# One start modulo 512 bytes for the matmul operands of a decoder layer, full-height compressed and last-block products, q and k turned before they are split

## The chip, the cores and the metric

The kernel runs on one core of a Trainium2 chip. The metric is the device time of one execution in microseconds (us); the lower the better. Times called ns are thousandths of that.

## The reference, cut to what matters

One layer works on 512 tokens of width 1024. The attention has 16 heads of 64, two key/value groups, and three branches: compressed blocks, selected blocks and a window. Both the selected and the window branch cover all earlier tokens at this length, so they are causal attentions with their own keys and values.

```
h = rms_norm(x, attn_norm_w);  z = h @ w_in
q, k = rope(rms_norm(q)) * SCALE, rope(rms_norm(k))       # by head, 64 wide
k_cmp, v_cmp = compress(k_c), compress(v_c)               # 31 blocks of 32 tokens
o = g0 * softmax(q k_cmp) v_cmp + g1 * softmax(q k_s) v_s + g2 * softmax(q k_w) v_w
x = x + (merge0 * (pool(u) @ w_pool_br) + merge1 * (o @ w_attn_br)) @ w_o
c = conv3(rms_norm(x, ffn_norm_w) @ w_up)                 # causal, per channel, 5504 wide
x = x + (silu(c[:2752]) * c[2752:]) @ w_down
```

## The kernel before, in words

Every fp32 product is made of rounded parts. `split` writes `hi`, the operand rounded to fp32r (ACT), and `lo`, the rest (DVE or POOL); `mm3` then runs three matmuls into one PSUM bank, `hi hi`, `hi lo` and `lo hi`, on lines 107 to 109. Transposes are matmuls of an fp32 tile with the identity `pk`.

The weights come through a ring: SP loads a 128x1024 tile `st` (2 buffers), ACT and DVE split it into 512-column tiles `hi` and `lo` (6 buffers each), TensorE (PE) uses them. All loads stand on SP's queue in program order, and each waits there until its buffer is free.

The stages, by the time at which they run:

- start to 40 us: x is loaded and split (`hh`, `hl`), the first 304 columns (`ka`), the norm.
- to about 180 us: token-major products `tg` of 256 columns for two k/v groups (`kv_group`) and four q groups (`q_group`), four token tiles each; pool mixer products `fm`, `pl`, `pb`; the compression (`ct`, `hp`, `kp`).
- to 394 us: attention, `scores` (`ss`) and `values` (`tp`, `op`) by head and branch, with the matmuls of 14 further weight tiles `fm` filled in between.
- to 441 us `w_ab` on the attention output `oT`; to 493 us `w_o` on `mh`, `ml`; to 743 us 43 tiles of `w_up` on `h2h`, `h2l` (`conv_tile`); then eight column blocks of `w_down` (`dn`) on `gh`, `gl`, with the last 64 rows of the weights kept apart (`gs`, `wlh`, `wll`).

The work of one q tile (`head_norm_rope`, `q_group`): ACT scales and squares the product, DVE and POOL make the norm and the rotation, DVE multiplies (L301). ACT writes a rounded copy into `qd` (L357), DVE the rest (L358); then PE turns four 128x128 blocks, one for each head with its two parts, into a bank `qt` of two (L361), and ACT and DVE copy two heads each out of it (L364, L365). The k tiles go the same way with four blocks (L344).

The compressed branch's product of a head has 32 rows in the contraction, in the strip of the array that the head's number sets, and runs twice, once for each part of the weights `pc` (L709):

```
for part in range(2):
    last = pe.matmul(op, Vc[32 * r:32 * r + 32, G], pc.out[part][32 * r:32 * r + 32], start=False,
                     stop=part == 1)
```

In the last block of `w_down`, L843 has all 128 rows and L844 has 64:

```
pe.matmul(ps[:, cs], wlh[:, sl], gs[:, cs], start=False, stop=False)
pe.matmul(ps[:, cs], wll[:64, sl], gs[:64, cs], start=False, stop=True)
```

Where the operands start in a partition's bytes, modulo 512 (a matmul's stationary operand and its moving one): `fm` of the early stages and of the attention 32 and 0; `w_ab` 32 and 32; `w_o` 32 and 480; `w_up` 32 and 0; `dn` 32 and 32; `tg` 0 and 32; `ss` 32 and 32; `op` 32 and 480; compressed `op` 416 and 480.

The order on each engine is set by a scheduler that goes by its own estimate of times; each engine takes its instructions in that order.

Of the kernel before, what the change touches and what calls it, by code (L numbers as in the profile page):

```python
# [19 lines left out]
P = 128  # L20
# [22 lines left out]
NKEEP = _OFF["cos"][0]  # L43

# [30 lines left out]
def layer(ctx: ExitStack, tc: tile.TileContext, par, masks, xT, w_kva, w_tm, w_fm, w_pl, w_pbr,  # L75
# [92 lines left out]
    pl_ = p1.tile([P, NPAR - NKEEP], F32, name="pl_")  # L168
# [7 lines left out]
    conv = pv("conv").rearrange("p (t c) -> p t c", c=4)  # L176
# [50 lines left out]
    for k in range(KC):  # L227
# [14 lines left out]
        if k == KC - 1:  # L242
            nc.sync.dma_start(pl_, par[:, NKEEP:])
# [38 lines left out]
    def head_norm_rope(ps, n, t, tab):  # L282
# [18 lines left out]
        v.tensor_tensor(y_, y_, rs[:, :n].unsqueeze(2).to_broadcast([P, n, DH]), ALU.mult)  # L301
        return y_
# [26 lines left out]
    def kv_group(b):  # L329
        for t, ps in tok_gemm(tm_weights(b), 256):  # L330
# [4 lines left out]
            kr = head_norm_rope(heads(ps[:, 0:128]), 2, t, 2 + b)  # L335
# [138 lines left out]
    def cmp_out(i):  # L474
# [20 lines left out]
        else:  # L495
# [6 lines left out]
            split(Vc[:, :, 0:DH], Vc[:, :, DH:P], heads(kp[:, :P]))  # L502
# [92 lines left out]
    class Cmp:  # L595
# [42 lines left out]
    work = {}  # L638

# [300 lines left out]
```

## Time and profile before

| | |
|---|---|
| time, median of 3 runs | 856.42 us (856.03 to 857.04) |
| the profiled execution's own time | 855.8 us |
| its span in the profile | 853.9 us |
| PE busy | 837.8 us, 4355 matmuls |
| DVE, ACT, POOL busy | 566.4, 466.5, 235.5 us |
| mean granted clock of PE | 0.996 |

PE's busy time counts the modelled end of each matmul, and matmuls overlap; what one costs in a stream is read from the distance of the starts, not from its duration. The span is the profile's time from the first to the last instruction.

### The profile page before, as it was taken

To read this page: it belongs to the slowest core of one execution; us is meant where nothing else is said; L and a number is where in the kernel's file an instruction comes from. 1 tells how busy PE (TensorE), PEld (TensorE's weight loads), DVE (VectorE), ACT (ScalarE), POOL (GpSimd) and SP (SyncE) were. 2 spreads that over 40 slices of the span, in tenths; PEclk is the share of its full clock that TensorE was granted. 3 is DMA by queue.
4 is the path that set the end of the run, shared out by engine and by line. 5 is a ranking of instruction groups with operands and counts; after the bars stand their busy time and mean duration, and the time that the engine had idled before them with its cause. 6 is when DMAs were issued, how large, how long until landed. Compare 5 with 4: busy or idle time off the path is not lost.

```text
span 853.9 us, 12252 instructions
## 1 busy us (share of the span) xinstructions
PE 837.8 (98%) x4355; PEld 700.9 (82%) x4355; DVE 566.4 (66%) x1203; ACT 466.5 (55%) x1002; POOL 235.5 (28%) x325
## 2 busy tenths in 40 slices
PE   7999899999999999999999999999999999999998
PEld 6889888978888888888888888888888888887887
DVE  7788967777787878785555539777777777423221
ACT  6846857768787877874334437545444444322220
POOL 5796714357565655640001200000000000000000
PEclk9999989999999999999999999999999999999999
DMA  6332132321001100101443223332233323333430
GB/s 218 102 119 91 51 102 96 103 96 50 26 26 47 30 25 26 47 28 50 148 148 99 98 74 100 99 98 83 91 100 98 99 85 104 111 108 99 111 98 25
DMA packets 22972, 72.82 MB, mean 85 GB/s; under 512 B 2816, under 2 KB 3328, under 8 KB 22912
## 3 DMA queue, kind: packets, MB, share of 16 engines
q1 hardware_dynamic: 22912, 72.05, 27.5%
q8 instruction: 34, 0.56, 0.3%
q14 instruction: 26, 0.21, 0.1%
HBM read 69.94 MB, written 2.10 MB: 84 GB/s over the span
## 4 chain that ended last, share of the span: by engine, by line
PE 84%; ACT 2%; DVE 1%; issue 1%; ACTq 0%; DVEq 0%
PE fm L107 16%; PE fm L108 16%; PE fm L109 16%; PE dn L107 5%; PE op L704 5%; PE dn L108 4%; PE dn L109 4%; PE tp L697 4%; PE ss L665 2%; PE ss L666 2%; PE op L709 1%; PE sc L608 1%; PE tg L312 1%; PE hp L461 1%; PE tg L310 1%; PE tg L311 1%
## 5 line engine op out<-in xcount | busy, mean ns | idle before, releaser
L95 ACT ACTIVATE hi<-st 128x512 fp32r<-128x512 f32 (+3 forms) x253 | 152.1, 607 | 202.2 <-PE fm L108 103.6
L98 DVE TENSOR_TENSOR lo<-st,hi 128x512 fp32r<-128x512 f32 (+1 forms) x210 | 141.8, 680 | 108.5 <-ACT hi L95 104.6
L107 PE MATMUL fm<-h2h,hi 128*128 128x512 f32 x344 | 136.1, 396 | 0.0
L108 PE MATMUL fm<-h2l,hi 128*128 128x512 f32 x344 | 136.0, 396 | 0.0
L109 PE MATMUL fm<-h2h,lo 128*128 128x512 f32 x344 | 135.9, 395 | 0.0
L677 POOL TENSOR_TENSOR pb<-pb,sm 128x128 f32<-128x128 f32 (+3 forms) x128 | 90.4, 738 | 49.3 <-DVE sm L674 40.4
L655 ACT ACTIVATE pb<-pb,nm 128x384 f32<-128x384 f32 (+3 forms) x128 | 71.1, 556 | 20.0 <-DVE nm L654 19.3
L107 PEld LDWEIGHTS fm<-h2h,hi 128*128 128x128 f32 x344 | 64.6, 188 | 15.7
L108 PEld LDWEIGHTS fm<-h2l,hi 128*128 128x128 f32 x344 | 64.6, 188 | 15.5
L109 PEld LDWEIGHTS fm<-h2h,lo 128*128 128x128 f32 x344 | 64.6, 188 | 15.5
L107 PE MATMUL fm<-hh,hi 128*128 128x512 f32 x160 | 71.6, 448 | 0.0
L107 PE MATMUL dn<-gh,hi 128*128 128x512 f32 (+1 forms) x189 | 69.9, 370 | 0.0
L108 PE MATMUL dn<-gl,hi 128*128 128x512 f32 (+1 forms) x189 | 69.1, 365 | 0.0
L109 PE MATMUL dn<-gh,lo 128*128 128x512 f32 (+1 forms) x189 | 69.1, 365 | 0.0
L98 DVE TENSOR_TENSOR ptl<-tp,pth 128x512 fp32r<-128x512 f32 (+1 forms) x96 | 57.2, 597 | 14.4 <-ACT pth L95 13.9
L654 DVE CUSTOM_DVE_ANT_0 pb<-ss,mk 128x384 f32<-128x384 f32 (+3 forms) x128 | 59.5, 482 | 8.5 <-PE ss L666 4.3
L108 PE MATMUL fm<-hl,hi 128*128 128x512 f32 x160 | 63.6, 397 | 0.0
L109 PE MATMUL fm<-hh,lo 128*128 128x512 f32 x160 | 63.0, 396 | 0.0
L95 ACT ACTIVATE pth<-tp 128x512 fp32r<-128x512 f32 (+1 forms) x96 | 49.8, 518 | 20.1 <-PE tp L697 19.7
L98 POOL TENSOR_TENSOR lo<-st,hi 128x512 fp32r<-128x512 f32 x36 | 48.5, 1350 | 34.4 <-ACT hi L95 34.4
L310 PE MATMUL tg<-hi,hh 128*128 128x256 f32 x192 | 54.1, 284 | 1.1 <-ACT h L288 1.1
L311 PE MATMUL tg<-hi,hl 128*128 128x256 f32 x192 | 53.6, 282 | 0.0
(256 smaller groups left out, 1838.4 us busy)
## 6 DMA issues: line engine op xcount, KB each, us to landing
st<-in_w_up SPq DMA_DIRECT2D x43, 512.0 KB, 3.5
st<-in_w_dn SPq DMA_DIRECT2D x24, 448.0 KB, 3.4
st<-in_w_fm SPq DMA_DIRECT2D x20, 512.0 KB, 3.5
st<-in_w_tm SPq DMA_DIRECT2D x12, 512.0 KB, 3.5
st<-in_w_ab SPq DMA_DIRECT2D x8, 512.0 KB, 3.4
st<-in_w_o SPq DMA_DIRECT2D x8, 512.0 KB, 3.5
x<-in_xT SPq DMA_DIRECT2D x15, 256.0 KB, 3.7
st<-in_cw SPq DMA_DIRECT2D x4, 512.0 KB, 3.7
```

Of the source, the lines that this page charges most:

```text
L95: a.activation(hi, src, AF.Copy)
L98: (eng or v).tensor_tensor(lo, src, r32(hi), ALU.subtract)
L107: pe.matmul(ps, sh, mh_, start=first and i == 0, stop=False)
L108: pe.matmul(ps, sh, ml_, start=False, stop=False)
L109: pe.matmul(ps, sl, mh_, start=False, stop=last and i == n - 1)
L310: pe.matmul(ps[:, :n], hh[k][:, tt], H, start=k == 0, stop=False)
L311: pe.matmul(ps[:, :n], hl[k][:, tt], H, start=False, stop=False)
L654: v.tensor_tensor_reduce(p_, ps, mcaus[:, S - n:], -1.0, 3e38, ALU.add, ALU.min, nm_[:, i:i + 1])
L655: a.activation(p_, p_, AF.Exp, bias=nm_[:, i:i + 1], scale=-1.0, accum_out=sm[:, i:i + 1])
L677: g.tensor_tensor(pb[:, PBASE[i]:PBASE[i] + n], pb[:, PBASE[i]:PBASE[i] + n], sm[:, i:i + 1].to_broadcast([P, n]), ALU.mult)
L697: last = pe.transpose(tp[:, n:n + P], pb[:, PBASE[i] + j * P:PBASE[i] + (j + 1) * P], ident)
L704: pe.matmul(op[:, j * P:], V2[b][j][:, G], pt_[:, TBASE[j]:TBASE[j] + w], start=b == 0 and j == 0 and part == 0, stop=False)
```

## The change

Tiles are placed in memory in another order, and `conv` leaves the constants' tile, so that both operands of nearly all wide matmuls start at 352 modulo 512: `tg`, `fm`, `pb`, `ss`, `op`, `w_ab`, `w_o`, `w_up` and `dn` have 352 and 352. Left elsewhere are the compressed branch (`pc` 480 on `Vc` 352; three of four windows of `Kc`), `hp`, `pl` and the identity.

`conv` is a tile of its own, loaded when the memory of the mixer is free. `Vc` gets 128 rows for each parity of the head, zero in the rows of other heads, and `pc` holds for a pair of heads the rounded part and the rest in one tile, so that a head has one matmul of 128 rows. `wll` and `gs` are used with all 128 rows. q and k are turned as fp32, two blocks for four heads (or for k's two groups), and split after it; the q bank now takes two token tiles.

```diff
 _PAR = [
-    ("ident", 128), ("fn", 8), ("psc", 4), ("conv", NFT * 4), ("b1", 2), ("vrow", 1),
+    ("ident", 128), ("fn", 8), ("psc", 4), ("b1", 2), ("vrow", 1),
     ("cos", 128), ("sin", 128), ("nw", 256), ("pos", 32), ("icnt", 64),
+    ("conv", NFT * 4),
 ]
...
     cp = pool(ctx, "cp")
+    ypp = pool(ctx, "ypp")
     xp = pool(ctx, "xp")
-    ypp = pool(ctx, "ypp")
...
+    Vc = kvp.tile([P, 2, 2, P], F32R, name="Vc")
+    g.memset(r32(Vc), 0.0)
     Kc = kvp.tile([P, 608], F32R, name="Kc")
     g.memset(r32(Kc), 0.0)
-    Vc = kvp.tile([P, 2, P], F32R, name="Vc")
...
-        v.tensor_tensor(y_, y_, rs[:, :n].unsqueeze(2).to_broadcast([P, n, DH]), ALU.mult)
-        return y_
+        rb = rs[:, :n].unsqueeze(2).to_broadcast([P, n, DH])
+        if out is None:
+            v.tensor_tensor(y_, y_, rb, ALU.mult)
+            return y_
+        o, form = out
+        v.tensor_tensor(o, form(y_), form(rb), ALU.mult)
...
-            HL = pp.tile([P, 2, 2, 2, DH], F32R, tag="kq", name=nm("kd"), bufs=KQ)
-            krb = kr[:, 0:2].unsqueeze(2).to_broadcast([P, 2, 2, DH])
-            a.activation(HL[:, 0], krb, AF.Copy)
-            v.tensor_tensor(HL[:, 1], krb, r32(HL[:, 0]), ALU.subtract)
+            k2 = pp.tile([P, 2, 2, DH], F32, tag="kq", name=nm("kd"), bufs=KQ)
...
-            for j in range(2):
-                for G in range(2):
-                    o = (2 * j + G) * P
-                    pe.transpose(tp[:, o:o + P], r32(HL[:, j, G]).rearrange("p a d -> p (a d)"), ident)
-            a.activation(KHL[:, b].rearrange("p j G s -> p (j G) s")[:, :, t * P:(t + 1) * P],
-                         tp.rearrange("p (c q) -> p c q", q=P), AF.Copy)
+            for G in range(2):
+                pe.transpose(tp[:, G * P:(G + 1) * P], k2[:, G].rearrange("p a d -> p (a d)"), ident)
+            tt = slice(t * P, (t + 1) * P)
+            split(KHL[:, b, 0, :, tt], KHL[:, b, 1, :, tt], tp[:, :2 * P].rearrange("p (G q) -> p G q", q=P))
...
-            qr = head_norm_rope(heads(ps[:, :256]), 4, t, 0)
-            d2 = pp.tile([P, 4, 2, DH], F32R, tag="kq", name=nm("qd"), bufs=KQ)
-            a.activation(d2[:, :, 0], qr, AF.Copy)
-            v.tensor_tensor(d2[:, :, 1], qr, r32(d2[:, :, 0]), ALU.subtract)
-            tp = bank_t("qt")
-            for h in range(4):
-                pe.transpose(tp[:, h * P:(h + 1) * P], r32(d2[:, h]).rearrange("p a d -> p (a d)"), ident)
...
-            a.activation(qp[0][:, :, tt], t4[:, 0:2], AF.Copy)
-            v.tensor_copy(qp[1][:, :, tt], t4[:, 2:4])
+            q2 = pp.tile([P, 2, 2, DH], F32, tag="kq", name=nm("qd"), bufs=KQ)
+            head_norm_rope(heads(ps[:, :256]), 4, t, 0,
+                           (q2.rearrange("p b a d -> p a b d"),
+                            lambda x: x.rearrange("p (a b) d -> p a b d", b=2)))
+            if t % 2 == 0:
+                tp = bank_t("qt").rearrange("p (b q) -> p b q", b=2)
+            o = t % 2 * P
+            for b in range(2):
+                pe.transpose(tp[:, b, o:o + P], q2[:, b].rearrange("p a d -> p (a d)"), ident)
+            if t % 2:
+                tt = slice((t - 1) * P, (t + 1) * P)
+                for a_ in range(2):
+                    rh, rl = slice(64 * a_, 64 * a_ + 64), slice(64 - 64 * a_, 128 - 64 * a_)
+                    a.activation(qp[a_][rh, :, tt], tp[rh], AF.Copy)
+                    v.tensor_tensor(qp[a_][rl, :, tt], tp[rh], r32(qp[a_][rh, :, tt]), ALU.subtract)
...
-            split(Vc[:, :, 0:DH], Vc[:, :, DH:P], heads(kp[:, :P]))
+            for r in range(4):
+                rr = slice(32 * r, 32 * r + 32)
+                split(Vc[rr, r % 2, :, 0:DH], Vc[rr, r % 2, :, DH:P], heads(kp[rr, :P]))
...
-            split(self.out[0], self.out[1], tps)
+            for j in range(2):
+                rh, rl = slice(64 * j, 64 * j + 64), slice(64 - 64 * j, 128 - 64 * j)
+                a.activation(self.out[j][rh], tps[rh], AF.Copy)
+                v.tensor_tensor(self.out[j][rl], tps[rh], r32(self.out[j][rh]), ALU.subtract)
...
-        for part in range(2):
-            last = pe.matmul(op, Vc[32 * r:32 * r + 32, G], pc.out[part][32 * r:32 * r + 32], start=False,
-                             stop=part == 1)
+        last = pe.matmul(op, Vc[:, r % 2, G], pc.out[r // 2], start=False, stop=True)
...
+    pq.tile([P, 32], F32, name="pqpad")
...
+    wlh = fp.tile([P, 1024], F32R, name="wlh")
+    wll = fp.tile([P, 1024], F32R, name="wll")
+    conv = fp.tile([P, NFT, 4], F32, name="conv")
+    nc.sync.dma_start(conv, par[:, NCONV:].rearrange("p (t c) -> p t c", c=4))
...
-            pe.matmul(ps[:, cs], wll[:64, sl], gs[:64, cs], start=False, stop=True)
+            pe.matmul(ps[:, cs], wll[:, sl], gs[:, cs], start=False, stop=True)
```

The order of instructions changes with it. The first place is PE where the first q group ends: the turned blocks `qt`, the pool mixer's `pl` and the compression's first product `hp` meet there. Before:

```order
L107 MATMUL pl_1435<-pli_913,plw_1409 128x512
L108 MATMUL pl_1435<-pli_913,plw_1409 128x512
L109 MATMUL pl_1435<-pli_913,plw_1410 128x512
L361 MATMUL qt_1351<-pk,qd_1348 128x128 x4
L361 MATMUL qt_1401<-pk,qd_1398 128x128 x4
L461 MATMUL hp_1664<-hi_1667,X_1140 128x256 x2
L461 MATMUL hp_1664<-lo_1672,X_1140 128x256 x2
L461 MATMUL hp_1664<-hi_1677,X_1140 128x256 x2
```

Eight transposes, the blocks of two token tiles in two banks, stand in a row ahead of `hp`. The same place on PE now:

```order
L319 MATMUL tg_1558<-hi_1419,hh_127 128x256
L320 MATMUL tg_1558<-hi_1419,hl_135 128x256
L321 MATMUL tg_1558<-lo_1420,hh_127 128x256
L371 MATMUL qt_1317<-pk,qd_1301 128x128 x2
L371 MATMUL qt_1317<-pk,qd_1345 128x128 x2
L109 MATMUL pl_1387<-pli_848,plw_1368 128x512
L110 MATMUL pl_1387<-pli_848,plw_1368 128x512
L111 MATMUL pl_1387<-pli_848,plw_1369 128x512
```

They are four now, in one bank, and stand ahead of `pl`; behind `pl` comes `hp`, in two halves with four more transposes between them.

The second place is PE at the end of the first head's values, where `op` takes the compressed branch before the next `tp`. Before:

```order
L665 MATMUL ss_2998<-KHL,qp_1187 128x256
L666 MATMUL ss_2998<-KHL,qp_1187 128x256
L704 MATMUL op_2730<-ptl_2802,V_143 128x256
L709 MATMUL op_2730<-pc_2683,Vc 128x512
L709 MATMUL op_2730<-pc_2684,Vc 128x512
L697 MATMUL tp_2885<-pk,pb_2767 128x128 x4
```

Two matmuls of 32 rows follow the 256-column one. Now, on PE:

```order
L691 MATMUL ss_2909<-KHL,qp_1164 128x256
L692 MATMUL ss_2909<-KHL,qp_1164 128x256
L729 MATMUL op_2643<-ptl_2715,V_143 128x256
L733 MATMUL op_2643<-pc_2596,Vc 128x512
L722 MATMUL tp_2797<-pk,pb_2682 128x128 x4
```

One matmul is gone; its neighbours are the same.

The third place is SP's queue of loads where the FFN begins, now:

```order
L155 DMA st_6022<-in_w_up 128x1024
L155 DMA st_6067<-in_w_up 128x1024
L155 DMA st_6108<-in_w_up 128x1024
L821 DMA conv<-in_par 128x172
L155 DMA st_6153<-in_w_up 128x1024
```

The load of `conv` is new there, behind the seventh tile of `w_up`; the other loads keep their order.

## Rows read from the trace of the kernel before

**Rows 1.** The page: the chain that ended last, shares of the span by engine.

```profile
PE 84%; ACT 2%; DVE 1%; issue 1%; ACTq 0%; DVEq 0%
```

**Rows 2.** Busy us (and count) of PE, PEld, DVE, ACT, POOL; PEclk; DMA, by stage.

```profile
40.00:120.00 80.00, 74.21 (x521) 68.55 (x522) 71.09 (x165) 51.24 (x135) 52.56 (x87) 0.96 0.31 96
181.00:394.00 213.00, 211.63 (x1212) 177.86 (x1210) 166.28 (x494) 159.47 (x421) 123.45 (x154) 1.00 0.12 36
493.00:743.00 250.00, 250.00 (x1081) 201.70 (x1079) 177.19 (x266) 121.83 (x183) 0.00 (x0) 1.00 0.31 95
```

**Rows 3.** Timeline of PE, start and duration in us: streams of `w_ab`, `w_o`, `w_up`.

```profile
399.77 0.39 PE L107 MATMUL fm<-oT,hi 128*128 128x512 f32 x1
...
405.89 0.39 PE L107 MATMUL fm<-oT,hi 128*128 128x512 f32 x1
...
444.75 0.39 PE L107 MATMUL fm<-mh,hi 128*128 128x512 f32 x1
...
450.35 0.39 PE L107 MATMUL fm<-mh,hi 128*128 128x512 f32 x1
...
599.80 0.40 PE L107 MATMUL fm<-h2h,hi 128*128 128x512 f32 x1
...
605.40 0.40 PE L107 MATMUL fm<-h2h,hi 128*128 128x512 f32 x1
```

**Rows 4.** Timeline of PE: 256 columns in `dn`; transposes and `tg` at 101 us.

```profile
836.10 0.28 PE L108 MATMUL dn<-gl,hi 128*128 128x256 f32 x1
...
838.98 0.28 PE L108 MATMUL dn<-gl,hi 128*128 128x256 f32 x1
...
101.42 0.60 PE L361 MATMUL qt<-pk,qd 128*128 128x128 f32 x4
...
101.97 0.28 PE L311 MATMUL tg<-hi,hl 128*128 128x256 f32 x1
...
102.44 0.28 PE L312 MATMUL tg<-lo,hh 128*128 128x256 f32 x1
```

**Rows 5.** Timeline of PE around a head's compressed product.

```profile
207.60 0.28 PE L704 MATMUL op<-ptl,V 128*128 128x256 f32 x1
207.80 0.73 PE L709 MATMUL op<-pc,Vc 32*128 32x512 f32 x2
208.47 0.66 PE L697 MATMUL tp<-pk,pb 128*128 128x128 f32 x4
```

**Rows 6.** Timeline of PE at the end of a `w_down` block.

```profile
742.91 0.39 PE L843 MATMUL dn<-gs,wlh 128*128 128x512 f32 x1
743.23 0.50 PE L844 MATMUL dn<-gs,wll 64*128 64x512 f32 x1
743.65 0.50 PE L107 MATMUL dn<-gh,hi 128*128 128x512 f32 x1
743.99 0.39 PE L108 MATMUL dn<-gl,hi 128*128 128x512 f32 x1
```

**Rows 7.** PE's wait at 104 us (timeline), and the stretch behind it, as Rows 2.

```profile
106.71 1.54 PE L361 MATMUL qt<-pk,qd 128*128 128x128 f32 x6 [2.59 <-DVE qp L365]
...
107.00:113.00 6.00, 5.24 (x24) 4.77 (x23) 5.93 (x15) 4.51 (x12) 0.71 (x2) 0.50 0.53 175
```

**Rows 8.** Groups of DVE instructions by form: busy us, mean ns, idle before.

```profile
L358 DVE TENSOR_TENSOR qd<-h,qd 128x256 fp32r<-128x256 f32 x16 | 8.5, 532 | 1.4 <-ACT qd L357 1.3
L365 DVE CAST qp<-qt 128x256 fp32r<-128x256 f32 x16 | 6.5, 416 | 1.0 <-ACT qp L364 0.9
L718 DVE TENSOR_TENSOR of<-op,of 64x512 f32<-64x512 f32 x16 | 11.1, 694 | 7.4 <-ACT of L717 7.2
```

**Rows 9.** SP's issue of the seventh `w_up` load; first use of `conv`; landing of `pk`.

```profile
499.55 0.33 SPq L153 DMA_DIRECT2D st<-in_w_up  x1
...
509.25 0.82 ACT L800 ACTIVATE c<-u,pk 128x512 f32<-128x512 f32 x1 [2.15 <-DVE u L798]
...
pk<-in_par SPq DMA_DIRECT2D x1, 157.5 KB, 6.0
```

More of the change, by code (lines that the diff above doesn't have):

```diff
@@ L43 @@
 NKEEP = _OFF["cos"][0]
+NCONV = _OFF["conv"][0]
 PBASE = [0, 128, 384, 768]
@@ L167, in layer @@
     pk = cp.tile([P, NKEEP], F32, name="pk")
-    pl_ = p1.tile([P, NPAR - NKEEP], F32, name="pl_")
+    pl_ = p1.tile([P, NCONV - NKEEP], F32, name="pl_")
     def pv(n):
@@ L175, in layer @@
     fn, psc, b1 = pv("fn"), pv("psc"), pv("b1")
-    conv = pv("conv").rearrange("p (t c) -> p t c", c=4)
     eps = cp.tile([P, 1], F32, name="eps")
@@ L242, in layer @@
         if k == KC - 1:
-            nc.sync.dma_start(pl_, par[:, NKEEP:])
+            nc.sync.dma_start(pl_, par[:, NKEEP:NCONV])
         split(hh[k], hl[k], xs, (an_ if k else an)[:, k:k + 1])
@@ L280, in layer, with head_norm_rope @@
     mcaus, mcmp = mk[:, :S], mk[:, S:]
-    def head_norm_rope(ps, n, t, tab):
+    def head_norm_rope(ps, n, t, tab, out=None):
         def sc():
@@ L334, in kv_group @@
             v.scalar_tensor_tensor(V2[b][t][:, :, DH:P], vin, rstd[:, t:t + 1], r32(vh), ALU.mult, ALU.subtract)
-            kr = head_norm_rope(heads(ps[:, 0:128]), 2, t, 2 + b)
-            HL = pp.tile([P, 2, 2, 2, DH], F32R, tag="kq", name=nm("kd"), bufs=KQ)
-            krb = kr[:, 0:2].unsqueeze(2).to_broadcast([P, 2, 2, DH])
-            a.activation(HL[:, 0], krb, AF.Copy)
-            v.tensor_tensor(HL[:, 1], krb, r32(HL[:, 0]), ALU.subtract)
-            tp = bank_t("kt")
-            for j in range(2):
-                for G in range(2):
-                    o = (2 * j + G) * P
-                    pe.transpose(tp[:, o:o + P], r32(HL[:, j, G]).rearrange("p a d -> p (a d)"), ident)
-            a.activation(KHL[:, b].rearrange("p j G s -> p (j G) s")[:, :, t * P:(t + 1) * P],
-                         tp.rearrange("p (c q) -> p c q", q=P), AF.Copy)
+            k2 = pp.tile([P, 2, 2, DH], F32, tag="kq", name=nm("kd"), bufs=KQ)
+            head_norm_rope(heads(ps[:, 0:128]), 2, t, 2 + b,
+                           (k2, lambda x: x.unsqueeze(2).to_broadcast([P, 2, 2, DH])))
+            tp = bank_t("kt")
+            for G in range(2):
+                pe.transpose(tp[:, G * P:(G + 1) * P], k2[:, G].rearrange("p a d -> p (a d)"), ident)
+            tt = slice(t * P, (t + 1) * P)
+            split(KHL[:, b, 0, :, tt], KHL[:, b, 1, :, tt], tp[:, :2 * P].rearrange("p (G q) -> p G q", q=P))
     QP = [None] * 8
@@ L354, in q_group @@
         for t, ps in tok_gemm(tm_weights(2 + gq), 256):
-            qr = head_norm_rope(heads(ps[:, :256]), 4, t, 0)
-            d2 = pp.tile([P, 4, 2, DH], F32R, tag="kq", name=nm("qd"), bufs=KQ)
-            a.activation(d2[:, :, 0], qr, AF.Copy)
-            v.tensor_tensor(d2[:, :, 1], qr, r32(d2[:, :, 0]), ALU.subtract)
-            tp = bank_t("qt")
-            for h in range(4):
-                pe.transpose(tp[:, h * P:(h + 1) * P], r32(d2[:, h]).rearrange("p a d -> p (a d)"), ident)
-            t4 = tp.rearrange("p (h q) -> p h q", q=P)
-            tt = slice(t * P, (t + 1) * P)
-            a.activation(qp[0][:, :, tt], t4[:, 0:2], AF.Copy)
-            v.tensor_copy(qp[1][:, :, tt], t4[:, 2:4])
+            q2 = pp.tile([P, 2, 2, DH], F32, tag="kq", name=nm("qd"), bufs=KQ)
[13 more added lines that the diff above has]
+                    v.tensor_tensor(qp[a_][rl, :, tt], tp[rh], r32(qp[a_][rh, :, tt]), ALU.subtract)
     def fm_tile(ws, ht, hl_):
@@ L635, in turn, with sums, turned @@
             self.out = [ap_.tile([P, S], F32R, tag=f"pc{j}", name=nm("pc")) for j in range(2)]
-            split(self.out[0], self.out[1], tps)
+            for j in range(2):
+                rh, rl = slice(64 * j, 64 * j + 64), slice(64 - 64 * j, 128 - 64 * j)
+                a.activation(self.out[j][rh], tps[rh], AF.Copy)
+                v.tensor_tensor(self.out[j][rl], tps[rh], r32(self.out[j][rh]), ALU.subtract)
     work = {}
+    def sums():
+        return [ap_.tile([P, NB], F32, tag=t, name=nm(t), bufs=4) for t in ("sm", "nm")]
+    def turned():
+        return [ap_.tile([P, NCAUS], F32R, tag=t, name=nm(t), bufs=2) for t in ("pth", "ptl")]
+    first = {"sm": sums(), "pt": turned()}
     def scores(u):
@@ L644, in scores @@
             for w in (u, u + 1):
-                work[w] = (ap_.tile([P, NCAUS], F32, tag="pb", name=nm("pb"), bufs=PBB),
-                           ap_.tile([P, NB], F32, tag="sm", name=nm("sm"), bufs=4),
-                           ap_.tile([P, NB], F32, tag="nm", name=nm("nm"), bufs=4))
+                sm, nm_ = first.pop("sm", None) or sums()
+                work[w] = ap_.tile([P, NCAUS], F32, tag="pb", name=nm("pb"), bufs=PBB), sm, nm_
         pb, sm, nm_ = work[u]
@@ L685, in values @@
         G, r = h // 8, h % 4
-        ph = ap_.tile([P, NCAUS], F32R, tag="pth", name=nm("pth"), bufs=2)
-        pl = ap_.tile([P, NCAUS], F32R, tag="ptl", name=nm("ptl"), bufs=2)
+        ph, pl = first.pop("pt", None) or turned()
         if b == 0:
@@ L821, in layer @@
             split(gh[j - 1], gl[j - 1], cg)
-    wlh = fp.tile([P, 1024], F32R, name="wlh")
-    wll = fp.tile([P, 1024], F32R, name="wll")
     wls = wr.tile([P, 1024], F32, tag="st", name="wls", bufs=ring.bufs[0])
```

## The prediction

> **What bounds the kernel now.** I read the chain of waits first: 84% of the span is PE's own work, and no other engine has more than 2% [rows 1]. The stages say the same. In the attention PE is busy in 211.6 of 213 us, in the `w_up` stage in all of 250; DVE is next with 166.3 and 177.2 us, so it has about a fifth or more to spare [rows 2]. Only from 40 to 120 us is PE not the clear bound: it is busy in 74.2 of 80 us and DVE in 71.1, and the granted clock is 0.96 [rows 2]. So outside that stretch the time is a sum over PE's matmuls, and a change is worth what it takes from the distance between their starts. Those distances I took from the timeline of PE.
>
> **What the operands' starts are worth.** Three streams of the same form (128 rows, 512 columns, stationary and moving both new at each matmul) differ in where their operands start. In `w_ab`, both at 32, 27 starts take 405.89 - 399.77 = 6.12 us: 226.7 ns each. In `w_o`, 32 against 480, 24 starts take 5.60 us: 233.3 ns. In `w_up`, 32 against 0, again 24 in 5.60 us: 233.3 ns [rows 3]. The dense streams that start alike are the faster ones by 6.6 ns, at either of two differences; by the code `w_ab` and `w_o` have the same splits of weights beside them. The change makes all of them start alike. It touches 43 x 24 = 1032 matmuls of `w_up`, 8 x 24 = 192 of `w_o`, and 20 x 24 = 480 early and in the attention (`fm` on `hh`): 1704 x 6.6 ns = 11.2 us.
>
> Against this stands `tg`, which also becomes alike. At 256 columns the equal start doesn't help: in `dn`, where both start at 32, 24 starts take 2.88 us or 120.0 ns, while four starts of `tg`, unlike by 32, take 102.44 - 101.97 = 0.47 us or 117.5 ns [rows 4]. 6 x 4 x 24 = 576 of them may lose 2.5 ns each, 1.4 us. Net gain of the placement: **9.8 us**, bounds 0 (other cause, below) and 11.2.
>
> There is a rule that speaks against this term. The Trainium skill (TensorE: Matmul & The Clock Gate, Part 2, step 1 of what a matmul does) says that the moving operand and the weight load have independent read ports, so that loading the next weights takes no read bandwidth from the running matmul; by that, where they start could not matter. The streams' 226.7 against 233.3 ns don't prove it wrong, since only the places differ that I know of; that is a rival below.
>
> **The compressed product.** From the last 256-column matmul of a head to the next `tp` it takes 208.47 - 207.60 = 0.87 us, with two 32-row matmuls between [rows 5]. A 256-column matmul in a stream takes 0.12 us [rows 4], so the pair costs 0.75 where two full-height ones would take 0.45 [rows 3]: the short ones are dear, and so is the step into them. One full-height matmul instead makes 0.12 + 0.23 = 0.35 us. 16 x 0.52 = **8.3 us**, all on PE's path. If the full-height one is no quicker to step into, only one start of 0.23 goes, and 3.6 us are left.
>
> The Trainium skill (same page, its closing table on why this matters for your kernels) holds that a 32-row matmul takes as long as a 128-row one. The trace of this kernel disagrees: 0.75 us for two in their surroundings against 0.45. By that rule the term would be 3.6 us, the lower bound just given from rows.
>
> **The last rows of `w_down`.** L843, L844 and the matmul behind them take 743.99 - 742.91 = 1.08 us [rows 6]; three in a full-height stream 0.68 [rows 3]. The 64-row one and both its neighbours pay. 0.40 us in eight blocks (the eighth in two halves, taken as one): **3.2 us**; at least 2, if only the two steps shown by L843 and L844 (0.74 against 0.45) go.
>
> **The transposes.** Four of them and one `tg` matmul take 101.97 - 101.42 = 0.55 us [rows 4]; less 0.12, 0.108 us each. The q tiles have 16 x 2 fewer, the k tiles 8 x 2: 48 x 0.108 = **5.2 us** of PE's work. Between 40 and 120 us part of it may only lengthen a wait; I let that be covered by the next term.
>
> **The work beside the transposes.** DVE loses, per q tile, the rest at 532 ns and a copy at 416 [rows 8]; instead there are two subtractions of 64 rows by 512 columns for two tiles, 694 ns each by the nearest row [rows 8]: 0.95 us become 0.69, 16 x 0.26 = 4.1 us. ACT loses a cast per tile in the same way. This pays where PE waits for DVE. The one large wait is 2.59 us at 104 us, for the copy out of a `qt` bank [rows 7]. Behind it the granted clock is 0.50, so 1.2 of 2.4 GHz, from 107 to 113 us, with PE busy in 5.24 of 6 us [rows 7]; at the full clock about half of that, 2.6 us, would not be spent. Together 5.2 us lie there. The wait needs not vanish: PE has the same order of things there, DVE is still nearly full, and a bank now takes two tiles and is released later. Bounds 0 and 5.2; I take a little under half, **2 us**.
>
> **What I cost at nothing.** `conv` is loaded behind the seventh `w_up` tile, which SP issues at 499.55 us; ACT first needs it at 509.25 [rows 9]. A load of 157.5 KB has taken 6.0 us to land [rows 9], and `conv` has 88 KB, so 9.7 us cover it with 3.7 to spare. Behind it on SP waits the next `w_up` tile, delayed by one issue of 0.33 us, and PE has several split tiles in hand. Uncovered, each us would come out of ACT's order, where the splits of the next weights wait behind the first `c`. The second split of `pc` for each four heads (694 ns more of DVE, and the like of ACT) and `Vc`'s four small splits lie under the attention, where DVE has 47 us free [rows 2]; uncovered they cost 4 x 1.4 = 5.6 us at most.
>
> **Sum.** 9.8 + 8.3 + 3.2 + 5.2 + 2 = 28.5 us from the profiled execution's 855.8 us: 827.3. That execution lies 0.6 us under the median of the runs shown, so the forecast is 828 us.
>
> **Rivals.**
>
> *The starts are worth nothing (0.14).* The 6.6 ns may come from what runs beside the streams; DVE is 71% busy in the `w_up` stage. Against it: `w_o` has `w_up`'s distance without `conv_tile`'s operations beside it, and `w_ab`, which also lacks them, the shorter one. Then 9.8 us stay: 838.
>
> *The early stage gives nothing back, or takes some (0.16).* The order of PE changes from the first products on, and DVE at 71 of 80 us sets the pace there. The transposes saved before 120 us and the 2 us go into waits: 831 to 834.
>
> *The wait at 104 us and its slow clock go altogether (0.15).* ACT and DVE are relieved of one step each between a q tile's last multiplication and its transposes, so the blocks may come in time: 828 - 3.2, or 825, and less where the small waits from 40 us on shrink too, 821.
>
> *Slower: paired transposes wait (0.03).* A `qt` bank is now full only with the second token tile, and its transposes stand in PE's order right behind the first's. If each of the eight pairs waits like the one at 104 us, 2.59 us, and drops the clock as that did, another 2.6, it is 8 x 5.2 = 42 us, and 869. It decides from 28 / 8 = 3.5 us a pair. Against it: the chain from DVE's multiplication to the transposes is shorter by two instructions, and from 120 us on PE has other products to run.
>
> **How the numbers follow.** The forecast as summed, within 4 us, has 0.52. The low end takes in the early stage's full gain, 820; the high end the starts without effect, 839, which holds about 0.85 of the chances. A measurement of this kernel can tell some 0.2%, 1.7 us, from no change. Only the last rival, and mishaps of its size, lead there or above: faster 0.96, same 0.01, slower 0.03.
>
> **What would show it.** Right: 24 starts of `w_up` in 5.44 us instead of 5.60, and the same in `w_o`; 0.35 us from the last 256-column matmul of a head to the next `tp`; L843's successors at 0.23 us each; no pause of PE before the first `c`. Open: whether the wait for a `qt` bank and the half clock behind it are still there. Wrong: `w_up` still at 233 ns, a wait of ACT for `conv`, or waits of PE between the two halves of a `qt` bank.

## The result, and the profile after

| | before | changed |
|---|---|---|
| time, median | 856.22 us (855.90 to 857.04) | 843.28 us (842.97 to 843.61) |
| ratio, 95% interval | | 0.985 (0.984 to 0.986) |
| span of the profiled execution | 853.9 us | 840.9 us |

Faster by 13 us, where 28.5 were forecast; 843.28 lies above the range of 820 to 839. The first matmul of each stage tells where the 13 us come from, and where the other 15 are missing. The forecast column is the prediction's sum laid out by stage: before the attention the transposes (5.2), the relief (2) and 6 of the 20 early `fm` tiles (1.0), less `tg`'s 1.4; in it the compressed product (8.3) and the other 14 tiles (2.2).

| stage | before, us | changed, us | gain | forecast |
|---|---|---|---|---|
| start to the first `ss` | 182.84 | 182.44 | 0.4 | 6.8 |
| attention | 214.88 | 213.54 | 1.3 | 10.5 |
| `w_ab` | 43.53 | 43.52 | 0.0 | 0 |
| `w_o` | 44.80 | 43.52 | 1.3 | 1.3 |
| `w_up` | 242.55 | 235.86 | 6.7 | 6.8 |
| `w_down` and the end | 125.30 | 122.02 | 3.3 | 3.2 |

From `w_ab` on every number came out to 0.1 us. Ahead of it 1.7 us came out of 17.3.

The chain of waits of the changed kernel, shares of the span by engine, shows the difference in one line:

```profile
PE 85%; DVE 7%; ACT 3%; DMA 2%; issue 1%; POOL 0%; SPq 0%; ACTq 0%; DVEq 0%; POOLq 0%
```

DVE had 1% of it [rows 1]. The windows of the same stages as [rows 2] (busy us of PE, PEld, DVE, ACT, POOL; PEclk; DMA):

```profile
40.00:120.00 80.00, 73.06 (x496) 67.12 (x496) 74.47 (x164) 48.81 (x123) 53.25 (x93) 0.96 0.32 96
181.00:394.00 213.00, 207.67 (x1200) 177.94 (x1201) 172.16 (x501) 162.07 (x429) 124.00 (x154) 0.99 0.11 35
483.00:733.00 250.00, 250.00 (x1110) 207.06 (x1109) 180.49 (x271) 124.89 (x187) 1.29 (x1) 1.00 0.31 98
```

(By the first matmul of each stage, `w_up` ran from 486.05 to 728.60 us before, so the last window of [rows 2], like the last one here, also holds 14 us of `w_down`.) In the `w_up` stage PE is as full as before. In the attention's window it now stands idle for 5.3 of 213 us, where it was 1.4, and DVE does 6 us more; counted from the first `ss` on, PE's idle time is 4.4 against 0.6 us. From 40 to 120 us DVE is busier than PE.

What answers to [rows 3 to 6], in the timeline of PE (start and duration): streams of `w_o` and `w_up`, a stream of `tg`, a head's compressed product, the last rows of `w_down`:

```profile
449.70 0.39 PE L109 MATMUL fm<-mh,hi 128*128 128x512 f32 x1
...
455.14 0.39 PE L109 MATMUL fm<-mh,hi 128*128 128x512 f32 x1
...
589.68 0.39 PE L109 MATMUL fm<-h2h,hi 128*128 128x512 f32 x1
...
595.12 0.39 PE L109 MATMUL fm<-h2h,hi 128*128 128x512 f32 x1
...
99.84 0.28 PE L319 MATMUL tg<-hi,hh 128*128 128x256 f32 x1
...
100.80 0.28 PE L321 MATMUL tg<-lo,hh 128*128 128x256 f32 x1
...
209.35 0.28 PE L729 MATMUL op<-ptl,V 128*128 128x256 f32 x1
209.47 0.40 PE L733 MATMUL op<-pc,Vc 128*128 128x512 f32 x1
209.71 0.60 PE L722 MATMUL tp<-pk,pb 128*128 128x128 f32 x4
...
733.16 0.39 PE L869 MATMUL dn<-gs,wlh 128*128 128x512 f32 x1
733.39 0.39 PE L870 MATMUL dn<-gs,wll 128*128 128x512 f32 x1
733.62 0.39 PE L109 MATMUL dn<-gh,hi 128*128 128x512 f32 x1
```

24 starts take 5.44 us in `w_o` and in `w_up` now, as forecast; the stage of `w_ab` is unchanged. Eight starts of `tg` take 0.96 us, 120 ns each, also as forecast. The compressed product takes 0.36 us between its neighbours instead of 0.87, and L869 and L870 are followed at 0.23. So these prices that the prediction took off PE were right (the one of the early `fm` was not; see below). What PE saved ahead of `w_ab` was for the most part not saved by the kernel, since there something else set the pace.

Two waits of PE show it, one at the end of the early stage and one in the attention. First PE, then DVE, then the granted clock behind it (PEclk is the last but two of the window's numbers):

```profile
176.38 2.12 PE L622 MATMUL sc<-qp,Kc 128*128 128x512 f32 x8
181.89 0.90 PE L629 MATMUL scq<-pk,cst 128*128 128x128 f32 x4 [3.39 <-DVE cst L624]
```

```profile
177.93 0.69 DVE L377 TENSOR_TENSOR qp<-qt,qp 64x512 fp32r<-64x512 f32 x1 [0.66 <-ACT qp L376]
178.66 0.69 DVE L521 TENSOR_TENSOR zg<-fm,rstdb 128x512 f32<-128x512 f32 x1
179.27 0.27 DVE L100 TENSOR_TENSOR Vc<-kp,Vc 32x128 fp32r<-32x128 f32 x1
180.10 0.69 DVE L527 SCALAR_TENSOR_TENSOR yp<-zg,yp 128x512 f32<-128x512 f32 x1 [0.57 <-ACT zg L522]
180.83 0.28 DVE L100 TENSOR_TENSOR Vc<-kp,Vc 32x128 fp32r<-32x128 f32 x1
181.15 0.69 DVE L624 TENSOR_TENSOR cst<-sc,mk 128x512 f32<-128x512 f32 x1
```

```profile
182.20:185.60 3.40, 3.40 (x13) 2.82 (x11) 2.10 (x7) 1.76 (x6) 0.00 (x0) 0.50 0.20 82
```

PE had the scores of the first compressed group ready at 178.5 us. DVE adds the mask to them (`cst`) only at 181.15, behind the last q subtraction, `zg`, `yp` and two of `Vc`'s four small splits. PE waits 3.39 us, and then runs at a granted clock of 0.50, so 1.2 of 2.4 GHz, for 3.4 us.

```profile
246.62 0.69 DVE L654 TENSOR_TENSOR pc<-pct,pc 64x512 fp32r<-64x512 f32 x1
247.34 0.69 DVE L741 TENSOR_TENSOR of<-op,of 64x512 f32<-64x512 f32 x1
248.06 0.69 DVE L100 TENSOR_TENSOR ptl<-tp,pth 128x512 fp32r<-128x512 f32 x1
248.67 0.17 DVE L699 RECIPROCAL sm<-sm 128x4 f32<-128x4 f32 x1
248.88 1.19 DVE L700 TENSOR_TENSOR sm<-sm,gt 128x4 f32<-128x4 f32 x1
250.09 0.69 DVE L654 TENSOR_TENSOR pc<-pct,pc 64x512 fp32r<-64x512 f32 x1
```

```profile
250.84 0.44 PE L722 MATMUL tp<-pk,pb 128*128 128x128 f32 x2 [0.39 <-DVE pc L654]
```

Here the second half of `pc`, whose cost was put at nothing, stands behind `of`, `ptl` and `sm` in DVE's order, 3.5 us after the first. Its bank `pct` is one of the two that `tp` uses, and PE's next transposes wait for it. With the shorter waits beside it PE stands idle for 1.2 us at this turn. The same comes back at 301 and 352 us.

### The profile page after: what moved, and what is told of

Same layout as the page of the kernel before. It is cut to its first block, busy times and chain, and to the rows that moved or that the text cites. A ratio compares the mean times of both kernels' runs of the same rounds, so it can differ in the third digit from the quotient of the medians.

```text
span 840.9 us, 12107 instructions
## 1 busy us (share of the span) xinstructions
PE 817.7 (97%) x4291; PEld 696.8 (83%) x4291; DVE 571.4 (68%) x1194; ACT 464.4 (55%) x985; POOL 233.7 (28%) x326
## 4 chain that ended last, share of the span: by engine, by line
PE 85%; DVE 7%; ACT 3%; DMA 2%; issue 1%; POOL 0%; SPq 0%; ACTq 0%; DVEq 0%; POOLq 0%
PE fm L109 16%; PE fm L111 16%; PE fm L110 16%; PE op L729 5%; PE dn L109 5%; PE dn L111 5%; PE dn L110 5%; PE tp L722 4%; PE ss L691 2%; PE ss L692 2%; PE tg L321 2%; PE tg L319 2%; PE tg L320 2%; DMA st<-in_w_fm 1%; PE pb L109 1%
## 5 line engine op out<-in xcount | busy, mean ns | idle before, releaser
L100 DVE TENSOR_TENSOR lo<-st,hi 128x512 fp32r<-128x512 f32 (+1 forms) x210 | 145.2, 695 | 100.5 <-ACT hi L97 99.2
L109 PE MATMUL fm<-h2h,hi 128*128 128x512 f32 x344 | 134.0, 389 | 0.0
L110 PE MATMUL fm<-h2l,hi 128*128 128x512 f32 x344 | 133.8, 389 | 0.0
L111 PE MATMUL fm<-h2h,lo 128*128 128x512 f32 x344 | 133.7, 389 | 0.0
```

The costliest lines, as they stand in the source:

```text
L100: (eng or v).tensor_tensor(lo, src, r32(hi), ALU.subtract)
L109: pe.matmul(ps, sh, mh_, start=first and i == 0, stop=False)
L110: pe.matmul(ps, sh, ml_, start=False, stop=False)
L111: pe.matmul(ps, sl, mh_, start=False, stop=last and i == n - 1)
```

## The experiments

The first four undo parts of the change, to see in which stage each part pays. In the tables of stages below, "first `ss`" and "attention" are read as in the table above, from one profiled execution of each kernel; that execution is 1.7 us under its kernel's median for ring_off, 1.3 over it for old_turn and 2.4 over it for best2, and within 0.5 us of it for the others.

**place_only.** The old q and k tiles, compressed product and last rows of `w_down`; left are the places in memory and `conv` as a load of its own. Beside the edits of the next two:

```diff
-            pe.matmul(ps[:, cs], wll[:, sl], gs[:, cs], start=False, stop=True)
+            pe.matmul(ps[:, cs], wll[:64, sl], gs[:64, cs], start=False, stop=True)
```

> The kernel before with the new placement alone: q and k turned as before, the compressed product as before, L844's product with 64 rows. Theory A (what PE saves counts in every stage): 9.8 us off, 846.4 us. Theory B (up to the end of the attention, saved PE time goes into waits for DVE's order; after it, it counts): only the 1224 matmuls of w_o and w_up pay, 1224 x 6.6 ns = 8.1 us, so 848.1 us, and the first row of w_ab comes within 1 us of where it was, 397.7 us.

**old_turn.** The changed kernel with q and k split before they are turned, as before.

```diff
-            k2 = pp.tile([P, 2, 2, DH], F32, tag="kq", name=nm("kd"), bufs=KQ)
+            HL = pp.tile([P, 2, 2, 2, DH], F32R, tag="kq", name=nm("kd"), bufs=KQ)
...
+            a.activation(HL[:, 0], krb, AF.Copy)
+            v.tensor_tensor(HL[:, 1], krb, r32(HL[:, 0]), ALU.subtract)
```

> The changed kernel with q and k split before they are turned, as before. Theory A: the 48 transposes and DVE's work come back, 843.3 + 7.2 = 850.5 us. Theory B: within 1.5 us of 843.3 us, since the first ss stood at 182.8 us before and 182.4 us after.

**old_pc.** The changed kernel with the compressed product in two 32-row matmuls.

```diff
-        last = pe.matmul(op, Vc[:, r % 2, G], pc.out[r // 2], start=False, stop=True)
+        for part in range(2):
+            last = pe.matmul(op, Vc[32 * r:32 * r + 32, G], pc.out[part][32 * r:32 * r + 32], start=False,
+                             stop=part == 1)
```

> The changed kernel with the compressed product as before (two matmuls of 32 rows a head, pc split in one piece of 128 rows). Theory A: 843.3 + 8.3 = 851.6 us. Theory B, with the two-part split of pc as what holds the attention up now: the attention as long as with the change, 213.6 us give or take 1.5, and 843 to 845 us; the waits of op and tp at about 250, 301 and 352 us are gone and the dear 32-row products are back.

**ring_off.** The changed kernel with the weight ring moved by 32 bytes, so that weights start at 384 and the other operand at 352.

```diff
     wr = pool(ctx, "wr")
+    wr.tile([P, 8], F32, name="wrpad")
```

> The changed kernel with 32 bytes put ahead of the weight ring, so that the stationary operands of w_o, w_up, tg and the early fm start at 384 and their moving ones at 352, and all else stays alike. If the start sets the distance: 24 starts of w_up take 5.60 us again, 843.3 + 8.1 = 851.4 us. If something else does: 5.44 us and 843.3 us.

| | median, us | ratio (95%) | first `ss` | attention | `w_o` | `w_up` | `w_down` |
|---|---|---|---|---|---|---|---|
| place_only | 851.57 | 0.995 (0.993 to 0.996) | 187.12 | 214.58 | 43.52 | 235.86 | 125.37 |
| old_turn | 845.72 | 0.988 (0.987 to 0.990) | 187.97 | 212.22 | 43.52 | 235.86 | 122.02 |
| old_pc | 846.01 | 0.989 (0.987 to 0.990) | 182.92 | 215.87 | 43.52 | 235.86 | 122.02 |
| ring_off | 851.38 | 0.995 (0.993 to 0.997) | 182.36 | 212.24 | 44.80 | 242.56 | 122.03 |

Of these expectations only ring_off's came true. The times of place_only, old_turn and old_pc lie in neither theory's range.

ring_off settles the placement after the attention: 32 bytes between the operands' starts give back exactly the old 44.80 and 242.56 us. old_pc puts the compressed product at 2.3 us of attention instead of 8.3. old_turn shows that turning unsplit gains 5.5 us before the attention (of which 1.3 may be its profiled execution's own), and yet the first `ss` comes only 0.4 us earlier than before, since place_only starts it 4.3 us later.

The attention of old_turn and of ring_off is 1.3 us shorter than the changed kernel's, and neither has a half clock at its start. In ring_off PE has the changed kernel's order and also waits for `cst`, but in its profiled execution the granted clock stays at 1.00 behind the wait, so 1.3 us is what the half clock costs there:

```profile
181.95 0.66 PE L630 MATMUL scq<-pk,cst 128*128 128x128 f32 x4 [3.47 <-DVE cst L625]
```

```profile
182.20:185.60 3.40, 3.40 (x20) 2.92 (x19) 2.58 (x11) 1.94 (x7) 0.00 (x0) 1.00 0.20 81
```

Those 4.3 us show up first on ACT. Its timeline of before, and then of place_only's and the changed kernel's row for `sr`, the square root of the norm:

```profile
20.15 0.63 ACT L95 ACTIVATE sh<-ssum 128x512 fp32r<-128x512 f32 x1 [2.76 <-DVE ssum L212]
21.40 1.15 ACT L95 ACTIVATE hi<-st 128x512 fp32r<-128x512 f32 x2 [0.61 <-DMA st<-in_w_tm]
...
27.38 0.69 ACT L196 ACTIVATE sr<-nsum,eps 128x512 f32<-128x512 f32 x1
```

```profile
30.05 0.69 ACT L197 ACTIVATE sr<-nsum,eps 128x512 f32<-128x512 f32 x1
```

```profile
20.46 1.16 ACT L97 ACTIVATE hi<-st 128x512 fp32r<-128x512 f32 x2 [3.89 <-DMA st<-in_w_tm]
21.53 0.62 ACT L97 ACTIVATE sh<-ssum 128x512 fp32r<-128x512 f32 x1
...
26.93 1.15 ACT L97 ACTIVATE hi<-st 128x512 fp32r<-128x512 f32 x2 [1.39 <-DMA st<-in_w_fm]
...
29.39 0.69 ACT L197 ACTIVATE sr<-nsum,eps 128x512 f32<-128x512 f32 x1
```

With the smaller first load and the other places (which of the two does it was not tested) the scheduler has put two ring splits ahead of `sh`, and two more ahead of `sr`. The norm is 2 us late, 2.7 in place_only, whose profile also has 3.4 us of half clock from 7.25 us on, and everything that needs `rstd` with it. The next two test that.

**norm_first.** The changed kernel with the old order of ACT at the norm; `NI` holds the two activations that write `sh` and `sr`.

```diff
     def tm_weights(i):
+        if i == 0:
+            with tc.issue_after(NI[0].ins):
+                return ring(w_tm[:, i, :1024], 256, 4) + ring(w_tm[:, i, 1024:], 256, 4)
...
+        if gi == 0:
+            with tc.issue_after(NI[1].ins):
+                ws = ring(w_fm[gi], P, KC, PIW[gi] and g)
```

> The changed kernel, with the first ring splits of the K/V weights queued behind the norm's sh on ScalarE and the first pool weights' behind sr, which is how the kernel before has them (its order of the first 80 rows on TensorE, VectorE and ScalarE is then the old one but for the K and q steps). Theory A (the new layout let the scheduler put two ring splits ahead of the norm; the norm's row sr then comes 2 us late, 29.4 against 27.4 us, and this is what ate the gain before the attention): sr back at 27.4 us, first hss at 31.7, and the first score matmul 2 to 4 us earlier than 182.4, at 178.4 to 180.4; the time 839 to 841.5. Theory B (VectorE is nearly full in 40 to 120 us, 74.5 of 80, and sets the end of that stage whatever comes first): sr at 27.4 too, but the first score matmul at 182.4 and the time 843.

**place_norm.** place_only with the same two edits.

> The kernel with the placement alone (old turning of q and k, old compressed product, old last rows of w_down), and with the norm in its old place: every instruction on TensorE, VectorE, ScalarE and GpSimd in the order of the kernel before, only the addresses differ (and one load is cut in two). Theory A (the order cost the 4.3 us by which the placement alone reached the attention late): the first score matmul at 182.8 to 184.3 us (TensorE's 576 tg matmuls are 2.5 ns longer each, 1.4 us), the time 847.3 to 848.8. Theory B (the addresses themselves slow the early stage): 187.1 us again and 851.6.

The other two test why the second split of `pc` costs something. **pc_pool** and **pc_copy** copy the bank once and split from the copy; in pc_copy DVE makes the low halves, in pc_pool GpSimd (`g` in place of `v`).

```diff
+            pcf = ap_.tile([P, S], F32, tag="ce", name=nm("pcf"))
+            a.activation(pcf, tps, AF.Copy)
             for j in range(2):
...
-                a.activation(self.out[j][rh], tps[rh], AF.Copy)
-                v.tensor_tensor(self.out[j][rl], tps[rh], r32(self.out[j][rh]), ALU.subtract)
+                a.activation(self.out[j][rh], pcf[rh], AF.Copy)
+                v.tensor_tensor(self.out[j][rl], pcf[rh], r32(self.out[j][rh]), ALU.subtract)
```

> The changed kernel, with the turned compressed weights copied from their PSUM bank by one ScalarE instruction; the two high halves are then made by ScalarE and the two low halves by GpSimd from that copy, nothing by VectorE. Theory A (pc's second split stands in VectorE's order behind of, ptl and sm and holds one of the two banks of tag t until then; TensorE waits some 1.9 us at each of three turns, in 247 to 252, 299 to 303 and 349 to 354 us): these waits go, the attention takes 207.5 to 209 instead of 213.5, the time 837.5 to 839.5. Theory B (the waits come from the tp banks' own splits, which VectorE does later because it is full): the attention 212.5 to 213.5, the time 842 to 843.

> As pc_pool, but the two low halves stay VectorE's, from the copy: VectorE's work is that of the changed kernel, and only the PSUM bank is free sooner. Theory A (the bank): the attention 208 to 210, the time 838 to 840.5, within 1 us of pc_pool. Theory B (VectorE's time, not the bank): 213.5 and 843, as the changed kernel, while pc_pool is faster.

| | median, us | ratio (95%) | first `ss` | attention |
|---|---|---|---|---|
| norm_first | 840.78 | 0.982 (0.980 to 0.984) | 180.62 | 213.10 |
| place_norm | 848.24 | 0.991 (0.989 to 0.992) | 183.59 | 214.57 |
| pc_pool | 841.07 | 0.982 (0.981 to 0.984) | 183.83 | 210.95 |
| pc_copy | 841.08 | 0.982 (0.981 to 0.984) | 183.35 | 210.79 |

place_norm is theory A: with the old order on every compute engine 3.5 of the 4.3 us are gone, and 0.75 are left, less than `tg`'s 1.4. In the changed kernel the same order is worth 2.5 us of time, in the lower half of what A expected, and the first `ss` comes 0.2 us later than its range. `sr` is back at 27.16 us (place_norm) and 27.29 (norm_first).

pc_copy and pc_pool agree within 0.2 us in the attention though DVE has 5 us less to do in pc_pool. So it is the bank, not DVE's time. But they gain 2.6 to 2.75 us of the attention, about half of what was expected, and the first `ss` comes 0.9 to 1.4 us later, so the times, 841.1 us, lie between the ranges of the two theories: the wait of `tp` for `pc` is gone, and some 0.9 us are left at the turn, now as waits for the splits of `tp`'s own banks. The timeline of PE in pc_copy there:

```profile
251.06 0.50 PE L731 MATMUL op<-pth,V 128*128 128x512 f32 x1 [0.68 <-ACT pth L97]
251.79 0.50 PE L731 MATMUL op<-ptl,V 128*128 128x512 f32 x1 [0.22 <-DVE ptl L100]
```

The last four try to win back what was lost, by order alone.

**hi_first.** At the two places where a bank is split by halves (`pc` and the q pairs), ACT's two halves first, then DVE's two.

```diff
             for j in range(2):
+                a.activation(self.out[j][64 * j:64 * j + 64], tps[64 * j:64 * j + 64], AF.Copy)
+            for j in range(2):
                 rh, rl = slice(64 * j, 64 * j + 64), slice(64 - 64 * j, 128 - 64 * j)
-                a.activation(self.out[j][rh], tps[rh], AF.Copy)
                 v.tensor_tensor(self.out[j][rl], tps[rh], r32(self.out[j][rh]), ALU.subtract)
```

> The changed kernel with one thing in another order: at the two places where one bank is split in two steps by halves (pc, and the q pairs), ScalarE makes both high halves first and VectorE then both low ones back to back, instead of high, low, high, low. No instruction is added or removed. Theory A (in the changed kernel ScalarE's second half waits for VectorE's first low half of the same bank, 0.75 us at 177.31, and the second low half then falls behind of, ptl and sm in VectorE's order; this alternation, not VectorE's time, is what the second split of pc costs): the waits at 247 to 254, 299 to 304 and 349 to 354 us shrink, the attention takes 210 to 211 us as with the copy, the time 840 to 841. Theory B (the bank is held by the two splits whatever their order, only a copy frees it): 213 to 213.5 us and 842.5 to 843.3.

**tail.** norm_first, and the last `zg`, `yp` and the low halves of `Vc` behind `cst` on DVE; `late` holds the splits of `Vc`, all four high parts first.

```diff
             pcs[0].score()
             pcs[0].soft()
+            with tc.issue_after(pcs[0].cst.ins):
+                f_g0(NPRE - 1, ps_g0, ap_)
+                late.pop()()
```

> The kernel with the norm first (norm_first), and at the end of the early stage VectorE adds the mask to the first compressed scores (cst) before the last g0 tile's zg and yp and before the low halves of Vc, which it did before cst. Nothing is added or removed. Theory A (the 3.8 us in which TensorE waits for cst, 176.0 to 179.86 us there, and the half clock of 3.4 us after them are VectorE's order): the wait falls to 1 us or less, the first score matmul at 177.5 to 178.5 instead of 180.6, and with no half clock the attention loses another 1.4 us: the time 836 to 838. Theory B (the work put behind cst comes back as a wait in the attention, or the clock falls anyway): the first score matmul early too, but the time 839 to 841.

**best2.** tail and hi_first together.

> The changed kernel with all three orders: the norm ahead of the ring splits (norm_first), cst ahead of zg, yp and Vc's low halves (tail), and pc and the q pairs split high, high, low, low (hi_first). Nothing is added or removed. Theory A (what the changed kernel saves on TensorE was lost to the order of VectorE and ScalarE at these three places, and they add): 2.5 from the norm, 3 to 4 from the end of the early stage, 2 to 2.7 from pc: 833.5 to 836 us. Theory B (they overlap, since VectorE is nearly full before the attention): 837 to 840.

**fin_copy.** tail and pc_copy together.

> The kernel with the norm and cst first (tail, 837.56 us, attention 212.27) and pc split from one ScalarE copy of its bank (as in pc_copy, where the attention was 210.79 instead of 213.54). Theory A (the two losses are separate: the order in front of the attention, and the bank of pc in it): the first score matmul at 178 to 179 us, the attention 209 to 210, the time 834.3 to 835.5. Theory B (the attention is by then bound by something else, and what pc gives back is lost in other waits): the attention 211.5 to 212.5, the time 836.5 to 838.

| | median, us | ratio (95%) | first `ss` | attention |
|---|---|---|---|---|
| hi_first | 844.11 | 0.986 (0.985 to 0.988) | 185.51 | 211.55 |
| tail | 837.56 | 0.978 (0.977 to 0.980) | 178.50 | 212.27 |
| best2 | 837.92 | 0.979 (0.978 to 0.981) | 182.35 | 210.72 |
| fin_copy | 834.61 | 0.975 (0.974 to 0.976) | 177.68 | 209.27 |

tail is theory A. PE's wait for `cst` is 0.79 us, and no half clock follows it:

```profile
178.09 0.66 PE L648 MATMUL scq<-pk,cst 128*128 128x128 f32 x4 [0.79 <-DVE cst L643]
178.50 0.36 PE L710 MATMUL ss<-KHL,qp 128*128 128x256 f32 x1
```

hi_first missed, for a reason that neither theory had. Its attention is 2.0 us shorter, so the order alone gives most of what the copy gives there; but the other order of the q pairs moves PE's order too, and the wait at 104 us becomes one of 5.03 for a `qt` bank:

```profile
109.03 1.08 PE L371 MATMUL qt<-pk,qd 128*128 128x128 f32 x4 [5.03 <-DVE qp L378]
```

best2 inherits that: it waits 5.00 us at the same place, and its time lies in theory B's range. fin_copy, without it, adds its two parts as theory A says: 8.7 us less than the changed kernel, 21.4 less than the kernel before. It beats both.

## Why the prediction was wrong

**Placement: right in the dense streams of `w_o` and `w_up`, mis-sized ahead of them.** 9.8 us were forecast. `w_o` and `w_up` gave 8.0 of the 8.1 that lay there, and ring_off shows that the equal start is the cause; the rival "the starts are worth nothing" is out. So is, for these streams, what the prediction drew from the rule against it (the Trainium skill, TensorE: Matmul & The Clock Gate, Part 2, step 1), that where the operands start could not matter: 32 bytes change 24 starts from 5.44 to 5.60 us.

The 480 early products gave 1.3 us of their 3.2. place_norm has the order of the kernel before on PE, so the two can be compared matmul by matmul. From the start of an `fm` to the next start on PE the mean falls from 237.9 to 233.5 ns before the attention, and from 257.3 to 255.4 in it: 4.4 and 1.9 ns, where 6.6 were taken for both. So this term was too high in its price, and not lost to a wait. In the attention an `fm` stands between other matmuls for the most part; why the equal start is worth less there stays open. `tg` lost 1.1 us of the 1.4. In sum place_norm is 0.75 us later at the attention and 0.3 us shorter in it, where 0.4 later and 2.2 shorter were forecast.

**The last rows of `w_down`: right.** 3.3 us instead of 3.2, in all runs with that part.

**The compressed product: the price right, the gain lost.** In the heads after the last turn of `pc` nothing else waits. The timeline of PE in before, whose last rows are L709's, and in the changed kernel:

```profile
207.80 0.73 PE L709 MATMUL op<-pc,Vc 32*128 32x512 f32 x2
...
362.24 0.73 PE L709 MATMUL op<-pc,Vc 32*128 32x512 f32 x2
...
393.45 0.73 PE L709 MATMUL op<-pc,Vc 32*128 32x512 f32 x2
```

```profile
362.91 0.40 PE L733 MATMUL op<-pc,Vc 128*128 128x512 f32 x1
...
392.31 0.39 PE L733 MATMUL op<-pc,Vc 128*128 128x512 f32 x1
```

Three heads take 393.45 - 362.24 = 31.21 us before and 392.31 - 362.91 = 29.40 after: 0.60 us a head. The product itself has 0.51 of it (0.36 us instead of 0.87 between its neighbours), as forecast, and again not what the rule says by which a 32-row matmul takes as long as a 128-row one (the Trainium skill, same page, closing table). The twelve heads ahead of these take 362.24 - 207.80 = 154.44 us before and 362.91 - 209.47 = 153.44 after: 1.0 us, where twelve times 0.60 would be 7.2. In them too the product and the step into it take 6.3 us less of PE's time; 6.0 us come back as longer distances between the starts of `op`, `fm` and `ss`, which in the last three heads are as before. This is the step that failed: "the second split of `pc` [...] and `Vc`'s four small splits lie under the attention, where DVE has 47 us free". DVE's free time is no cover for an instruction that holds a bank and stands in DVE's order. The bound given there, 5.6 us, is near the 6.2 that went. With the bank free sooner (pc_copy) they take 360.81 - 211.10 = 149.71 us:

```profile
211.10 0.39 PE L735 MATMUL op<-pc,Vc 128*128 128x512 f32 x1
...
360.81 0.39 PE L735 MATMUL op<-pc,Vc 128*128 128x512 f32 x1
```

So the bank has 3.7 of the 6.2 us, of which 0.7 go again ahead of the first of these heads. The other 2.5 stay open: at the turn shown above they are waits for `pth` and `ptl`, and which order of ACT and DVE would remove them was not tried.

**"Outside that stretch the time is a sum over PE's matmuls."** This sentence carried the whole sum, and it holds only from `w_ab` on. In the attention PE was busy in 211.6 of 213 us [rows 2], but that doesn't say how far off the next limit is. With some 10 us less for PE to do (16 x 0.60) the order of ACT and DVE is that limit: 213.5 us, and 209.3 in the best kernel here. Of the 9.2 us missing in the attention the twelve heads have 6.2, the placement 1.9 and the half clock at its start 1.3, which is the whole within 0.2 us.

**The transposes and the relief: 5.5 us made, 5 lost again.** Forecast 5.2 and 2 us; old_turn shows 5.5, or 4.2 if its profiled execution's excess lies there. The rival "the early stage gives nothing back" came true, and in size too: 6.4 of 6.8 us were lost, and without the attention's loss the time would have been its 834. Its mechanism was half of it. Saved time did go into a wait for DVE, but at 178 us and not before 120. In the kernel before, `cst` stood behind `zg`, `Vc` and `yp` in DVE's order too; PE only came there later, at 181.65 us instead of 178.50, and hardly waited:

```profile
179.55 2.10 PE L608 MATMUL sc<-qp,Kc 128*128 128x512 f32 x8
182.43 0.66 PE L615 MATMUL scq<-pk,cst 128*128 128x128 f32 x4 [0.78 <-DVE cst L610]
```

With `cst` ahead of these the first `ss` comes 2.1 us earlier, and the attention is 0.8 us shorter without the half clock. The other half was a new delay, the norm behind ring splits (1.8 us at the first `ss`; 3.5 with the old q tiles). With both orders mended the first `ss` comes at 178.50 us, 4.3 earlier than before, which is the forecast's 6.8 without the 2 for the wait at 104 us, but for 0.5. The norm's place stood in the order of the changed kernel and could be read ahead of any run; the prediction read that order only at the places of its own terms.

**The wait at 104 us** is still there, but for another thing: not for a `qt` bank, but for DVE's part of the pool mixer's `plo`, in front of `hp`. The granted clock is 0.51 from 107 to 113.8 us there:

```profile
108.45 0.79 PE L473 MATMUL hp<-hi,X 128*128 128x256 f32 x2 [3.24 <-DVE plo L103]
```

The rival that it goes was wrong, and so were the 2 us taken for it. The rival "paired transposes wait" was wrong for the changed kernel; hi_first, with one other order of the halves, has such a wait of 5.03 us, once.

**Cost at nothing, rightly:** `conv`. It is issued at 498.73 us, lands 3.2 us later, and ACT's first use is at 505.8; PE has no wait there.

**What is left.** The best kernel here, 834.61 us, lies 6.6 us over the forecast of 828. By the figures above the 480 early `fm` have 1.9 of these, the wait at 104 us has 2, and 2.5 are the open part of the compressed product.

## What to carry to other kernels

Price a saving on the busiest engine stage by stage, and ask for each stage which engine's order is next: it is worth its full size only where the others have slack in their order, not only in their busy time. A distance read in a dense stream holds for dense streams: the 6.6 ns were 1.9 where the matmul stands among others. A split that is cut in two holds its bank until the second half's turn comes in the queue; copy the bank once, or put the halves together. After any change of sizes or places compare the order of all engines at the start and at the seams of stages, since a scheduler that goes by estimates may have moved the one chain that everything waits for.

## What the runs showed of the hardware

In the dense streams of `w_ab`, `w_o` and `w_up`, with both operands at one place modulo 512 bytes (32 and 32, 352 and 352) a 512-column matmul starts 226.7 ns after the last; 32 bytes apart (384 and 352) it is 233.3, as with 32 and 0 or 32 and 480. Among the other matmuls of the attention the step from 32 and 0 to 352 and 352 was worth 1.9 ns (place_norm). At 256 columns the equal start is the slower one, 120.0 against 117.5 ns.

In the changed kernel a wait of PE of 3.39 us was followed by 3.4 us at half clock, in tail one of 0.79 by none. The wait's length alone doesn't decide it: in ring_off one of 3.47 us at the same place was followed by none.

On DVE, a multiplication of 128x256 with one broadcast operand took 512 ns on average (`qd`), with two of them 760 (`kd`); what else differs between them was not tested. The groups of the changed kernel by form (busy us, mean ns, idle before):

```profile
L311 DVE TENSOR_TENSOR qd<-h,hrs 128x256 f32<-128x256 f32 x16 | 8.1, 512 | 0.2
L311 DVE TENSOR_TENSOR kd<-h,hrs 128x256 f32<-128x256 f32 x8 | 6.0, 760 | 0.1
```
